# Operand tiles of a two-layer decoder kernel moved to per-stage byte offsets

## The chip, the cores and the metric

The kernel runs on one core of a Trainium2 chip. The metric is the device time of one execution in microseconds. A core has five engines that run side by side: TensorE (matmuls), VectorE, ScalarE, GpSimd and SyncE (which here only issues transfers). The profile calls them PE (PEld for its weight loads), DVE, ACT, POOL and SP. Operands lie in SBUF, a memory of 128 partitions; TensorE writes its sums to PSUM.

## What is computed

Two layers of a decoder over 256 tokens of width 1024, in float32: a mixer block with four branches and gates, a cross attention over 256 memory tokens, and an MLP. Each is added to the residual x.

```python
def reference(x, mem, positions, norm_mix, w_in, ...):
    for l in range(DEPTH):
        h = rmsnorm(x, norm_mix[l])
        x = x + mixer_block(h, positions, w_in[l], ...)
        x = x + cross_attention(rmsnorm(x, norm_xattn[l]), rmsnorm(mem, norm_mem[l]),
                                xattn_wq[l], xattn_wk[l], xattn_wv[l], xattn_wo[l])
        x = x + squared_relu_mlp(rmsnorm(x, norm_mlp[l]), w_up[l], w_down[l])
    return rmsnorm(x, norm_final)

def mixer_block(h, ...):
    zin = h @ w_in
    ...
    proj = jnp.einsum('bsnw,nwd->bsnd', branches, w_branch)
    gate = jax.nn.sigmoid(gates).reshape(b, s, N_BRANCH, D_MODEL)
    merged = jnp.sum(gate * proj, axis=2)
    return merged @ w_out

def squared_relu_mlp(h, w_up, w_down):
    a = jax.nn.relu(h @ w_up)
    return (a * a) @ w_down
```

w_in has 6840 columns (2744 for the four branches and 4096 for the gates), w_up and w_down have 1024 x 4096 weights. Nearly all the work is products of the 256 tokens with these weights.

## The kernel before

**Activations and products.** Activations lie transposed: the channel on the partition, 256 tokens along it, two blocks of 128 channels in one tile of 128 x 2 x 256 floats (2048 bytes in a partition). Products are made to nearly float32 accuracy from three matmuls in a narrower format, float32r: each operand is split into a high part and the rest, and `mm3` (line 188) adds high x high, high x low and low x high into one PSUM bank. So for each block of 128 x 128 weights there are three matmuls with 256 columns, and each of them has its own weight load (LDWEIGHTS) ahead of it:

```python
def mm3(out, ah, al, bh, bl, start, stop):
    PE.matmul(out, ah, bh, start=start, stop=False)
    PE.matmul(out, ah, bl, start=False, stop=False)
    PE.matmul(out, al, bh, start=False, stop=stop)
```

In `gemm` (line 207) the weights are the stationary side and the activations move: one half of a weight transfer (128 x 1024) holds eight blocks, and is followed by 24 matmuls. In `gemm_tok` (line 237) the activations are stationary and the weights move, with 512 columns in a matmul; it is used for a part of w_in, for the cross attention's values and for the last product of the second layer.

**Weights.** `half` (line 166) takes half of a transfer of 1 MB from the buffers `wr` (three of them, issued by SyncE in order), lets ScalarE write the high part `wh` and VectorE the rest `wl`. There are four buffers of each, 4096 bytes in a partition.

**Operands.** The other side of each product is split in the same way and lies in tiles named by the stage: `xh`, `xl` (normed x for w_in), `hh`, `hl` (for the gates, for the queries and for the MLP's w_up), `mh`, `ml` (memory for keys and values), `brh`, `brl` (branches), `mgh`, `mgl` (merged, for w_out), `oh`, `ol` (attention, for the output weights), `ah`, `al` (the MLP's hidden layer, for w_down). Other products among tiles, `kx` with `qx` and `ph` with `vx` in the cross attention, and small products in full float32 (`cst` with `sq` in `stat`, line 340, among others) stand between the large ones.

**Where tiles lie.** Each pool is a stretch of SBUF, and the tiles of a pool follow each other. Pool `cp` has constants and x. Pool `wp` has three `wr` of 8192 bytes, then four `wh` and four `wl` of 4096. Pool `ap` begins with a pad of `PAD` = 48 floats (line 123), and then has only tiles of 2048 bytes: 44 pieces that `new` (line 88) hands out and `rel` takes back, eight tiles for gates (`gate_tile`, line 350, which also hold `xh` and `xl` of a layer's first product), and eight for `hh` and `hl`, made once in layer 0 (lines 1051 to 1054) and written anew for each of their three stages. At the bottom of SBUF, ahead of all pools, 16,384 bytes of each partition are kept by default for descriptors of transfers that GpSimd issues.

**Order.** In a layer the stages are: w_in (`ev_dn`, `zin_rest`), then the mixers, written as generators whose pieces alternate, while the gates' products follow (`gates`, line 1075); then the keys of the cross attention (`mh`), `merge` (`brh`), w_out (`mgh`), the queries (`hh`), the attention, its output product (`oh`), w_up (`hh`) and w_down (`ah`). A scheduler orders the instructions by the program's order and by raised priorities (`urgent`, `high_priority`); each engine then runs its own list and waits at semaphores. `operands` (line 353), called where a residual is added, writes the split operands of the stage that follows.

## Time and profile before

| | |
|---|---|
| runs | 1099.88 and 1101.76 us, median 1100.82 us |
| profiled execution | 1099.05 us |
| its span, first to last instruction | 1097.3 us |
| mean granted TensorE clock | 0.997 |
| busy: PE, PEld | 1072.7 us (98%), 1028.3 us (94%) |
| busy: DVE, ACT, POOL | 812.4 us (74%), 583.7 us (53%), 196.2 us (18%) |
| matmuls recorded | 8494 |
| transferred | 185.13 MB, mean 169 GB/s |

The page of a profile gives one execution: the busy time of each engine, the chain of work that ended last with its share by engine and line, the costliest groups of instructions (line, engine, operation, output and inputs by name, shape, count, busy time, mean duration, and the idle time ahead of them), and the transfers. Other views cut out windows of time, list instructions in order of time, or list who waited for whom. A name such as `g<-hh,wl` says that a PSUM tile `g` is written from the moving operand `hh` and the stationary operand `wl`. Matmuls overlap: the next one starts before the last one has ended, so a matmul's duration is longer than its share of the time.

### The profile page before, as it was taken

Reading aid. Unit: us, or ns where it says so; the run is one execution under the profiler, and the core shown is the slowest. Engines: PE = TensorE matmul, PEld = TensorE weight load, DVE = VectorE, ACT = ScalarE, POOL = GpSimd, SP = SyncE. Lnnn points to the kernel's source line nnn. Section 1 sums busy time; section 2 is a strip of 40 time slices with the busy share of each in tenths; the row PEclk is TensorE's granted clock in tenths of the full one; section 3 lists DMA queues with packets and bytes.
Section 4 is the critical chain, followed back from the end, with each engine's and each line's share of the span. In section 5 each row is a group of like instructions: output and inputs, shape, how many; then the busy total and the mean of one; then the engine's idle time right before and its main releaser. Section 6 shows DMA issues by size and latency. Waiting matters only on the chain.

```text
span 1097.3 us, 20696 instructions
## 1 busy us (share of the span) xinstructions
PE 1072.7 (98%) x8494; PEld 1028.3 (94%) x8494; DVE 812.4 (74%) x1419; ACT 583.7 (53%) x875; POOL 196.2 (18%) x170
## 2 busy tenths in 40 slices
PE   8989999999999999999999999999999999999996
PEld 8979998899998999999999899999999899999885
DVE  7999858789865966655679997586797778665454
ACT  6565554554654655544454746554455555555342
POOL 6334005108200200000101420320361001010000
PEclk9999999999999999999999999999999999999998
DMA  9442623354543555555555444244555345554551
GB/s 368 169 173 98 224 86 123 106 193 174 182 151 148 182 185 179 188 190 192 192 183 192 155 151 156 85 166 136 191 188 197 119 151 193 192 205 161 194 189 39
DMA packets 28319, 185.13 MB, mean 169 GB/s; under 512 B 3392, under 2 KB 3648, under 8 KB 6976
## 3 DMA queue, kind: packets, MB, share of 16 engines
q1 hardware_dynamic: 26208, 179.09, 45.0%
q10 hardware_dynamic: 2016, 4.72, 1.3%
q8 instruction: 66, 1.08, 0.4%
q14 instruction: 29, 0.24, 0.1%
HBM read 182.75 MB, written 1.05 MB: 168 GB/s over the span
## 4 chain that ended last, share of the span: by engine, by line
PE 80%; DVE 11%; ACT 3%; DMA 3%; issue 1%; POOL 1%; ACTq 0%; DVEq 0%; POOLq 0%
PE g L189 24%; PE g L191 24%; PE g L190 24%; DVE wl L185 3%; DMA mr<-memt 2%; DVE qt L846 1%; PE ps L189 1%; ACT wh L182 1%; PE ps L191 1%; PE ps L190 1%; DVE gt L1097 1%; PE ps L652 1%; PE ps L648 1%; DMA wr<-ws 1%; DVE mgl L1105 1%
## 5 line engine op out<-in xcount | busy, mean ns | idle before, releaser
L185 DVE TENSOR_TENSOR wl<-wr,wh 128x1024 fp32r<-128x1024 f32 (+1 forms) x337 | 416.0, 1237 | 188.3 <-ACT wh L182 186.7
L182 ACT ACTIVATE wh<-wr 128x1024 fp32r<-128x1024 f32 (+1 forms) x337 | 354.9, 1056 | 343.0 <-PE g L190 241.7
L191 PE MATMUL g<-hh,wl 128*128 128x256 f32 x1152 | 325.4, 283 | 3.5 <-DVE wl L185 3.5
L189 PE MATMUL g<-hh,wh 128*128 128x256 f32 x1152 | 324.1, 282 | 2.1 <-ACT gt L1082 1.5
L190 PE MATMUL g<-hl,wh 128*128 128x256 f32 x1152 | 323.2, 281 | 0.0
L191 PEld LDWEIGHTS g<-hh,wl 128*128 128x128 f32 x1152 | 217.0, 188 | 5.4 <-DVE wl L185 4.3
L189 PEld LDWEIGHTS g<-hh,wh 128*128 128x128 f32 x1152 | 217.2, 189 | 3.3 <-ACT gt L1082 2.0
L190 PEld LDWEIGHTS g<-hl,wh 128*128 128x128 f32 x1152 | 218.4, 190 | 0.4 <-issue 0.2
L329 POOL TENSOR_TENSOR sq<-sq,sq 128x512 f32<-128x512 f32 x14 | 22.1, 1580 | 350.0 <-ACT sq L321 349.8
L189 PE MATMUL g<-xh,wh 128*128 128x256 f32 x272 | 75.2, 281 | 1.2 <-ACT xh L302 1.2
L190 PE MATMUL g<-xl,wh 128*128 128x256 f32 x272 | 75.8, 281 | 0.3 <-DVE xl L311 0.3
L191 PE MATMUL g<-xh,wl 128*128 128x256 f32 x272 | 74.9, 280 | 0.0
L189 PE MATMUL g<-ah,wh 128*128 128x256 f32 x256 | 72.0, 281 | 0.0
L190 PE MATMUL g<-al,wh 128*128 128x256 f32 x256 | 72.0, 281 | 0.0
L191 PE MATMUL g<-ah,wl 128*128 128x256 f32 x256 | 72.0, 281 | 0.0
L189 PEld LDWEIGHTS g<-xh,wh 128*128 128x128 f32 x272 | 51.0, 189 | 1.6 <-ACT xh L302 1.6
L190 PEld LDWEIGHTS g<-xl,wh 128*128 128x128 f32 x272 | 51.2, 189 | 0.5 <-DVE xl L311 0.5
L1098 POOL TENSOR_TENSOR gt<-gt,gt 128x512 f32<-128x512 f32 x16 | 35.5, 2217 | 89.9 <-DVE gt L1097 89.0
L191 PEld LDWEIGHTS g<-xh,wl 128*128 128x128 f32 x272 | 50.8, 189 | 0.0
L191 PE MATMUL g<-wh,al 128*128 128x512 f32 x128 | 50.1, 394 | 0.0
L190 PE MATMUL g<-wl,ah 128*128 128x512 f32 x128 | 49.9, 392 | 0.0
L189 PE MATMUL g<-wh,ah 128*128 128x512 f32 x128 | 49.4, 389 | 0.0
(500 smaller groups left out, 2333.7 us busy)
## 6 DMA issues: line engine op xcount, KB each, us to landing
wr<-ws SPq DMA_DIRECT2D x166, 1024.0 KB, 4.8
wr<-ws ACTq DMA_DIRECT2D x4, 512.0 KB, 7.5
mr<-memt ACTq DMA_DIRECT2D x8, 256.0 KB, 4.7
par<-par SPq DMA_DIRECT2D x2, 778.0 KB, 7.0
x<-xt SPq DMA_DIRECT2D x3, 256.0 KB, 7.6
cst<-cst SPq DMA_DIRECT2D x1, 588.0 KB, 8.7
gf<-fin SPq DMA_DIRECT2D x2, 256.0 KB, 5.3
yt<-yg ACTq DMA_DIRECT2D x2, 256.0 KB, 2.5
```

The costliest lines, as they stand in the source:

```text
L182: i = S.activation(wh[:, p], r[:, p], AF.Copy)
L185: V.tensor_tensor(wl[:, p], r[:, p], wh[:, p].bitcast(F32), op=ALU.subtract)
L189: PE.matmul(out, ah, bh, start=start, stop=False)
L190: PE.matmul(out, ah, bl, start=False, stop=False)
L191: PE.matmul(out, al, bh, start=False, stop=stop)
L329: G.tensor_tensor(acc, acc, sq, op=ALU.add)
L648: PE.matmul(xp[:, h], M[:, h], Tm[:, h], start=True, stop=True)
L652: PE.matmul(up[:, h], X[t][:, h], U[:, h], start=True, stop=True)
L846: V.tensor_tensor(qt[:, a].rearrange("p (b h) -> p b h", h=h), e3, halves(qbd[a // 2][:, a % 2], i)[:, :, 1], op=ALU.mult)
L1097: V.scalar_tensor_tensor(gt[m][a], gt[m][a], 1.0, ps, op0=ALU.add, op1=ALU.mult)
L1098: G.tensor_tensor(gt[m][0], gt[m][0], gt[m][1], op=ALU.add)
L1105: V.scalar_tensor_tensor(dl, t, 0.5, dh.bitcast(F32), op0=ALU.mult, op1=ALU.subtract)
```

## The change

The change gives the operands of each stage a byte offset within their tile, from a table with one row per layer. To make room for it, each of the 60 tiles of pool `ap` (pieces, gate tiles and tiles of h) becomes 128 bytes longer, 2176 instead of 2048. The 7,680 bytes that this takes come from the reserve at the bottom of SBUF, which goes from 16,384 to 1,024 bytes.

- `place` makes a tile of 512 + 32 floats and returns a view of it that begins at the given byte.
- `new` and `gate_tile` look the name up in the row of the layer that `lay` holds; names that are not in the table begin at 0. Where before `xl` was a name of its own, both parts of x are now looked up as `xh`.
- `hplace` makes the eight tiles of h once and returns views at the offset of the stage: `gate` before the gates, `q` before the product whose residual writes the queries' operands, `up` before the one that writes those of w_up.
- `lay` is set at the start of a layer, and to the next layer just before w_down of layer 0, as its residual writes the next layer's `xh`.

No instruction is added to the program or taken from it.

```diff
+SLACK = 128
+PLACE = [
+    dict(xh=16, gate=112, mh=8, ml=8, brh=120, brl=120, mgh=32, mgl=32, q=96, oh=48, ol=48, up=16, ah=112, al=112),
+    dict(xh=112, gate=8, mh=16, ml=16, brh=112, brl=112, mgh=4, mgl=4, q=124, oh=64, ol=64, up=120, ah=16, al=16),
+]
...
+    lay = [0]
+
+    def place(dt, shape, tag, name, byte):
+        t = ap.tile([P, 512 + SLACK // 4], dt, tag=tag, name=name)
+        n = int(np.prod(shape[1:]))
+        v = t[:, byte // 4 : byte // 4 + n]
...
+        return v
+
     def new(dt=F32, shape=(P, 2, T), name="a"):
...
-        t = ap.tile(list(shape), dt, tag=f"pc{i}", name=nm(name))
+        t = place(dt, shape, f"pc{i}", nm(name), PLACE[lay[0]].get(name, 0))
...
+    hf, hv = [], {}
+
+    def hplace(stage):
+
+        if not hf:
+            for j in range(4):
+                hf.append([ap.tile([P, 512 + SLACK // 4], F32R, tag=f"h{n}{j}", name=nm("h" + n)) for n in "hl"])
+        o = PLACE[lay[0]][stage] // 4
+        for n in range(2):
+            hv[n] = [t[n][:, o : o + 512].rearrange("p (a b) -> p a b", a=2) for t in hf]
+        return hv[0], hv[1]
...
     def gate_tile(i, dt=F32, name="gt"):
-        return ap.tile([P, 2, T], dt, tag=f"gt{i}", name=nm(name))
+        return place(dt, (P, 2, T), f"gt{i}", nm(name), PLACE[lay[0]].get(name, 0))
...
-            dh, dl = (Norm.h[j], Norm.l[j]) if mix else (hh[j], hl[j])
+            dh, dl = (Norm.h[j], Norm.l[j]) if mix else (hv[0][j], hv[1][j])
...
-        if l == 0:
-            for j in range(4):
-                for d, n in ((hh, "hh"), (hl, "hl")):
-                    d.append(ap.tile([P, 2, T], F32R, tag=f"{n}{j}", name=nm(n)))
+        hh, hl = hplace("gate")
+        H, L = ch(hh), ch(hl)
...
+        hh, hl = hplace("q")
+        H, L = ch(hh), ch(hl)
         gemm(ch(mgh), ch(mgl), 8, 4, residual(gain(4 * l + 1)), lead=True, tail=True)
...
+        hh, hl = hplace("up")
+        H2, L2 = ch(hh), ch(hl)
         gemm(ch(oh), ch(ol), 8, 4, residual(gain(4 * l + 3)), lead=True, tail=True)
...
-        gemm(H, L, 8, 16, ev_up, lead=True)
+        gemm(H2, L2, 8, 16, ev_up, lead=True)
         if l + 1 < NL:
+            lay[0] = l + 1
             gemm(ch(ah), ch(al), 32, 4, residual(gain(4 * l + 4), True, rrow), tail=True)
...
-    nc = _bacc.Bacc("TRN2", target_bir_lowering=False, num_devices=1)
+    nc = _bacc.Bacc("TRN2", target_bir_lowering=False, num_devices=1, dynamic_dma_scratch_size=1024)
```

## The prediction

> **What bounds the kernel now.** I read the page first: engine totals, chain that ended last, costliest groups.

> ```profile
> span 1097.3 us, 20696 instructions
> ...
> PEclk9999999999999999999999999999999999999998
> ...
> PE 80%; DVE 11%; ACT 3%; DMA 3%; issue 1%; POOL 1%; ACTq 0%; DVEq 0%; POOLq 0%
> ...
> L191 PE MATMUL g<-hh,wl 128*128 128x256 f32 x1152 | 325.4, 283 | 3.5 <-DVE wl L185 3.5
> ```

> The reader is to see that TensorE carries the chain, at the full granted clock, and that its work is one kind of matmul: three per 128x128 block of weights (lines 189 to 191), 256 columns each. They number 3 x 1152 with h, by the loops 3 x 272 with xh, 3 x 256 with ah, and 384 each with mh, br, mg and oh: 6576. The wait view says how little else there is. Its largest rows are these, and all its rows make some 15 us.

> ```profile
> PE g L191 <- DVE wl L185: 3.5, 4, 1.0
> PE ps L693 <- DVE s L690: 1.6, 1, 1.6
> ```

> So the time is the number of matmuls times the step from one to the next. A duration of 283 ns is no step, since two or three matmuls are in flight. The step comes from the windows view (window, its length, TensorE's busy time and count): the length over the count less 2.4, for the matmuls that began before the window (283 over 118).

> ```profile
> 39.00:59.00 20.00, 20.00 (x172) 1.00 0.49 170
> 267.50:290.00 22.50, 22.50 (x192) 1.00 0.53 198
> 290.50:313.00 22.50, 22.50 (x194) 1.00 0.51 184
> 377.60:462.40 84.80, 84.80 (x723) 1.00 0.53 188
> 462.60:553.00 90.40, 90.40 (x770) 1.00 0.52 186
> 553.40:576.00 22.60, 22.60 (x194) 1.00 0.49 184
> 831.60:849.00 17.40, 17.40 (x150) 1.00 0.59 207
> 913.80:998.50 84.70, 84.70 (x722) 1.00 0.54 196
> 811.00:829.00 18.00, 18.00 (x161) 1.00 0.55 212
> 769.00:783.00 14.00, 14.00 (x126) 1.00 0.52 200
> 648.00:657.00 9.00, 9.00 (x82) 1.00 0.33 115
> 889.00:907.00 18.00, 18.00 (x161) 1.00 0.40 131
> 103.00:112.00 9.00, 9.00 (x79) 1.00 0.13 43
> 632.00:644.00 12.00, 12.00 (x104) 1.00 0.47 175
> 759.00:767.00 8.00, 8.00 (x70) 1.00 0.36 133
> 313.20:317.70 4.50, 4.50 (x40) 1.00 0.46 131
> 849.30:853.90 4.60, 4.60 (x41) 1.00 0.39 137
> 607.00:617.00 10.00, 10.00 (x45) 1.00 0.52 179
> 1001.00:1087.00 86.00, 86.00 (x377) 1.00 0.40 147
> ```

> The first eight rows (w_in of layer 0 late, w_out and q of layer 0, up, down, w_in of layer 1, q and up of layer 1) are one speed: 90.40 / (770 - 2.4) = 117.8 ns, 84.70 / (722 - 2.4) = 117.7; where the quotient is above that, a short wait is in it. The next four are another: 18.00 / (161 - 2.4) = 113.5, then 113.3, 113.1, 113.5; I call it 113.4. The three after them, in the mixer stages, are at the first speed again (117.5, 118.1, 118.3). The two rows of kx with qx are a third: 119.7 and 119.2. The last two, with 512 columns, come back in part (3). Clock and instruction are the same in all; only operands and history differ. The timeline shows where the speed changes:

> ```profile
> 375.87 0.28 PE L190 MATMUL g<-hl,wh 128*128 128x256 f32 x1
> 375.98 0.28 PE L191 MATMUL g<-hh,wl 128*128 128x256 f32 x1
> 376.10 0.50 PE L343 MATMUL ps<-cst,sq 128*128 128x1 f32 x4
> ...
> 376.89 0.28 PE L191 MATMUL g<-hh,wl 128*128 128x256 f32 x1
> 377.01 0.28 PE L190 MATMUL g<-hl,wh 128*128 128x256 f32 x1
> 377.13 0.28 PE L191 MATMUL g<-hh,wl 128*128 128x256 f32 x1
> ```

> Steps of 0.11 before four small products of the norm, of 0.12 after them, and then 117.8 through all of up and down. The speed is a pace (113.4 the quick one, 117.8 the long one) that lasts until something else runs on TensorE. The products come in threes, and three steps take 340, 353 and 359 ns: the quick pace plus none, two and three hitches of some 6.5 ns. [...]

> **The change, part by part.** In the kernel before, the sizes of the weight buffers and of the pieces are multiples of 128 bytes and the pad between them is 192, so every operand lies 64 bytes past such a multiple, counted from the weights. With the table the distance modulo 128 is 64 plus the entry. Layer 0: xh 80, gate 48, mh 72, br 56, mg 96, q 32, oh 112, up 80, ah 48. Layer 1: xh 48, gate 72, mh 80, br 48, mg 68, q 60, oh 0, up 56, ah 80. A piece of 2176 bytes is 17 x 128, and the smaller reserve at the bottom moves everything by 15,360 = 120 x 128 bytes; so tiles without an entry keep their distance, and kx with qx (both pieces, distance 0) stay at 119.7.

> What a new distance does to the step, no row shows. The bounds from rows are 113.4, the quick pace, and 119.7, distance 0. I take 113.4: distance 64 reaches it for whole stages, and is thrown out of it only by what comes between, so a distance that suits a stage needs only to keep it there.

> (1) The first eight rows hold 3117 matmuls, 3100 without those that began before. 3100 x (117.8 - 113.4) = 13.6 us, all on the path, as TensorE waits for nothing there. Bounds: that, or 3100 x (119.7 - 117.8) = 5.9 us lost.

> (2) The other 3476 alternate. Of the seven windows quoted of them (811 to 767 in the list, 88 us) three are at the long pace, 29 us: a third, so 1150 x 4.4 = 5.1 us. Some of it meets a wait; I take 4. Bounds: 5.1 won, or, from a mean of 114.9, 3476 x (119.7 - 114.9) = 17 us lost.

> (3) The matmuls in which the weights are the moving side have 512 columns: 86.00 / (377 - 1.7) = 229.1 ns in the last gemm (384 by its loop), 231 in the window of w_in of layer 1, which I take for all other 288. Twice the quick step is 226.8, so 0.9 + 1.2 = 2.1 us at best; nothing at worst, or the same lost again. I take 1.0.

> (4) oh of layer 1 goes to distance 0, that of kx with qx, and runs at the quick pace now (889 to 907). 192 x (119.7 - 113.5) = 1.2 us lost; 0 if the place keeps the quick pace.

> (5) No instruction is added: the place calls only make views, and the three places of h lie in the tiles that h had before, so the same waits order them. ScalarE and VectorE write the same elements from another start, under this cover (PE, PEld, DVE, ACT, POOL):

> ```profile
> 388.00:557.00 169.00, 169.00 (x1437) 169.00 (x1437) 103.73 (x106) 84.19 (x100) 6.44 (x5) 1.00 0.52 186
> ```

> VectorE is busy 61% of the densest stretch, ScalarE 50%, the DMA engines 52%. At 113.4 these become 64, 52 and 54%, no bound yet, and writes slower by a tenth would still leave TensorE the last. Large transfers all go through queues that SP and ACT issue, none by POOL, so I cost the smaller reserve at nothing:

> ```profile
> q1 hardware_dynamic: 26208, 179.09, 45.0%
> ...
> wr<-ws SPq DMA_DIRECT2D x166, 1024.0 KB, 4.8
> ```

> Were transfers slower for it, three buffers of two halves each stand against a landing of 4.8 us; one buffer lasts 48 x 113.4 ns = 5.4 us.

> Sum: -13.6 - 4 - 1.0 + 1.2 = -17.4 us. The profiled execution took 1099.05 us (span 1097.3 and 1.75 around it), 1.8 below the median of the runs shown. So 1081.7 on its scale, 1083 on that of the runs, which I take.

> **The rivals.**

> B, half of it. What comes between still throws stages into the long pace, though others than now. For it: w_out has the long pace in layer 0 (267 to 290) and the quick one in layer 1 (811 to 829), from the same code at the same distance. Half of 17.4 us: 1091.

> C, no effect. History alone decides, distance nothing; some stages swap paces, and the time stays within 4 us of 1100. For it: the same two rows. Against it: kx with qx, which lie at another distance, have another speed, the same in both layers. [...]

> D, slower. A start that is no multiple of 64 bytes costs each matmul one more hitch, the 119.7 step, whatever the pace. The mean step is now (3100 x 117.8 + 3476 x 114.9) / 6576 = 116.3, so with a share s at 119.7 and the rest at 113.4 the gain is gone at s = 2.9 / 6.3 = 0.46. With all there, 6576 x 3.4 = 22 us are lost, and 2 more in the 512-column stages: 1125. For it: every entry but that of oh in layer 1, 64, leaves the grid of 64 bytes, and no row shows such a start; against it: nothing. [...]

> E, below the quick step. 113.4 may hold a hitch itself, as the rungs 113.4, 117.8 and 119.7 need not begin with the lowest. One matmul in three without a hitch of 6.5 ns is 2.2 ns a step, 6576 x 2.2 = 14 us more: 1069; all of them without it, 1040. For it: only the spacing of the rungs. Against it: no quoted window of 256 columns is under 113.

> **How the numbers follow.** The forecast has 0.44, with a range of its own from 1077 (parts 1 to 3 at their best, no loss at oh) to 1088 (part 1 two thirds done); B 0.19, C 0.14, D 0.10, E 0.13. The range 1070 to 1101 leaves out D, most of E and the upper end of C. A measurement of this kernel tells about 2%, 22 us, from no change: below 1078.8 lie E and a quarter of the forecast, 0.24; above 1122.8 half of D, 0.05; the rest is 0.71.

> **What would show it.** The forecast: the windows of up, down and w_in of layer 1, now at 117.8, come out at 113.4, and the step is the same before and after the norm's four products. Part (4): oh of layer 1 at 119.7. Part (5): the DVE, ACT and DMA rows unchanged. B shows as stages at two speeds, others than now; C as a mean step of 116.3; D as 119 or more in most stages; E as any long window under 113. The ground of it is wrong if a stage's speed differs from piece to piece of one operand: neighbouring pieces, now 2176 bytes apart, alternate modulo 256, so that the pattern would repeat at 256 bytes and not at 128.

## The result and the profile after

The changed kernel takes 1113.04 us (1112.35 and 1113.73), against 1100.82: a ratio of 1.0111, 95% interval 1.0065 to 1.0157. It is a loss of about 12 us where the forecast had a gain of 17, and it lies above the range of the forecast, which ended at 1101. The number of instructions is the same, 20696. These are the lines of the page after; the line numbers have moved, and `mm3` is now at 218 to 220:

```profile
span 1110.4 us, 20696 instructions
...
PE 1088.0 (98%) x8494; PEld 1043.6 (94%) x8494; DVE 812.7 (73%) x1419; ACT 584.3 (53%) x875; POOL 195.9 (18%) x170
...
PE 88%; DVE 6%; ACT 2%; DMA 2%; issue 1%; POOL 0%; DVEq 0%; ACTq 0%
...
L220 PE MATMUL g<-hh,wl 128*128 128x256 f32 x1152 | 326.0, 283 | 3.2 <-DVE wl L214 3.2
...
wr<-ws SPq DMA_DIRECT2D x166, 1024.0 KB, 4.8
```

TensorE's busy time rose by 15.3 us for the same 8494 matmuls, and every other engine's total stayed within 0.7 us. The mean of one matmul, 283 ns, says nothing of it, as before. Nor did a large new wait appear; these are the two largest of TensorE's waits, and the same two cost 3.5 and 1.2 us before:

```profile
PE g L220 <- DVE wl L214: 3.2, 4, 0.8
PE g L218 <- ACT xh L331: 2.0, 1, 2.0
```

The whole time without a matmul, span less busy time, fell from 24.6 to 22.4 us. So the loss is in the step. The windows view of TensorE in the changed kernel shows it, read as in the prediction: the length over the count less 2.4 (1.7 in the last row, with 512 columns).

```profile
382.00:466.00 84.00, 84.00 (x715) 1.00 0.52 185
470.00:557.00 87.00, 87.00 (x738) 1.00 0.51 184
925.00:1009.00 84.00, 84.00 (x703) 1.00 0.51 184
815.00:834.00 19.00, 19.00 (x159) 1.00 0.50 174
225.00:245.00 20.00, 20.00 (x170) 1.00 0.57 203
892.00:916.00 24.00, 24.00 (x206) 1.00 0.35 121
838.00:857.00 19.00, 19.00 (x164) 1.00 0.46 168
653.50:662.50 9.00, 9.00 (x78) 1.00 0.26 97
318.00:322.00 4.00, 4.00 (x36) 1.00 0.32 100
1020.00:1100.00 80.00, 80.00 (x347) 1.00 0.40 145
```

The steps, in the order of the rows, with the step of the same stage in the kernel before in brackets: up of layer 0 117.9 ns (117.7), down 118.3 (117.8), up of layer 1 119.9 (117.7), w_out of layer 1 121.3 (113.5), keys of layer 0 119.3, oh of layer 1 117.9 (113.5), q of layer 1 117.6 (118), mixers 119.0 (113.1), kx with qx 119.0 (119.7), last product 231.7 (229.1). The granted clock is 1.00 in all of them, before and after. No stage has the quick pace any more.

The mean by stage can be had from the start times of all matmuls in the trace, from one start to the next (steps of 135 ns and more, in which something else stands between, are left out, and so are ten of under 30 ns). Over the 256-column matmuls it goes from 116.35 to 118.57 ns. Times the number of matmuls, the stages of the prediction's part (1) lose 4.6 us, the rest of the 256-column stages 11.0, of which oh of layer 1 has 0.9, and the 512-column ones 1.2. That makes 16.8; with 2.2 us less without a matmul 14.6 remain, against 13.1 in the span. The other 1.5 us I can't place.

### The profile page after: what moved, and what is told of

Read it like the earlier page. It is cut to its first block, busy times and chain, and to the rows that moved or that the text cites. A ratio compares the mean times of both kernels' runs of the same rounds, so it can differ in the third digit from the quotient of the medians.

```text
span 1110.4 us, 20696 instructions
## 1 busy us (share of the span) xinstructions
PE 1088.0 (98%) x8494; PEld 1043.6 (94%) x8494; DVE 812.7 (73%) x1419; ACT 584.3 (53%) x875; POOL 195.9 (18%) x170
## 3 DMA queue, kind: packets, MB, share of 16 engines
q1 hardware_dynamic: 26208, 179.09, 44.7%
## 4 chain that ended last, share of the span: by engine, by line
PE 88%; DVE 6%; ACT 2%; DMA 2%; issue 1%; POOL 0%; DVEq 0%; ACTq 0%
PE g L218 26%; PE g L219 26%; PE g L220 26%; DVE wl L214 2%; DMA mr<-memt 1%; PE ps L218 1%; PE ps L219 1%; PE ps L220 1%; DVE qt L875 1%; ACT wh L211 1%; PE ps L677 1%; PE ps L681 1%; DMA wr<-ws 0%; PE ps L986 0%; DVE sp L530 0%
## 5 line engine op out<-in xcount | busy, mean ns | idle before, releaser
L218 PE MATMUL g<-xh,wh 128*128 128x256 f32 x272 | 76.2, 284 | 2.0 <-ACT xh L331 2.0
L219 PE MATMUL g<-xh,wh 128*128 128x256 f32 x272 | 76.5, 283 | 0.0
L218 PEld LDWEIGHTS g<-xh,wh 128*128 128x128 f32 x272 | 51.4, 190 | 2.4 <-ACT xh L331 2.4
L219 PEld LDWEIGHTS g<-xh,wh 128*128 128x128 f32 x272 | 51.4, 189 | 0.1
## 6 DMA issues: line engine op xcount, KB each, us to landing
wr<-ws SPq DMA_DIRECT2D x166, 1024.0 KB, 4.8
```

## Experiments

The operands' distance from the weights' buffers is given below modulo 256 bytes where the tiles of pool `ap` lie a multiple of 256 apart. There the base (table entry 0) is 192, the same as in the kernel before, whose tiles are 2048 = 8 x 256 apart. Diffs are against the changed kernel. Each time is a median; each ratio is to the kernel before, run on the same chip.

### Spacing and offsets apart

The change does two things: tiles 2176 bytes apart instead of 2048, and offsets from a table. Three kernels take them apart. `spacing_2176` keeps the spacing, with all offsets 0:

```diff
-PLACE = [
-    dict(xh=16, gate=112, mh=8, ...
+ZERO = dict(gate=0, q=0, up=0)
+PLACE = [ZERO, ZERO]
```

> Tiles 2176 bytes apart as in the change, every offset of the table 0, so all operands stay 64 past a multiple of 128 from the weights. Theory S (the spacing does it: the pattern that decides the step repeats at 256 bytes or more, and neighbouring tiles that alternate break the quick pace): 1109 to 1114 us, no stage below 117 ns a step. Theory O (the offsets do it: a distance other than 64 modulo 128 takes the quick pace away): 1101 us within 4, w_out of layer 1 and oh at 113.4 as before, and kx with qx at 119.8.

`spacing_2304` makes the room 256 bytes as well, so that tiles are 2304 = 9 x 256 apart:

```diff
-SLACK = 128
+SLACK = 256
+ZERO = dict(gate=0, q=0, up=0)
+PLACE = [ZERO, ZERO]
```

> Tiles 2304 = 9 x 256 bytes apart, every offset 0. Theory S with a period of 256: as before the change, 1101 us within 4, with stages at 113.4 and 117.8. Theory S with a longer period (512 or more): 1107 to 1114, no stage at 113.4. Theory O: 1101 within 4.

`table_2304` keeps the offsets of the change, with tiles 2304 apart:

```diff
-SLACK = 128
+SLACK = 256
```

> The change with 256 instead of 128 bytes of room: its offsets, but tiles 9 x 256 bytes apart. Theory S with a period of 256: the gain that the offsets may bring is seen alone, under 1105 us, with stages at 113.4. Theory O: as the change, 1109 to 1116 us, steps of 117.8 to 121.5 by stage (121 for w_out of layer 1 at distance 68).

| kernel | tiles apart | offsets | us | ratio, 95% |
|---|---|---|---|---|
| spacing_2304 | 2304 | none | 1099.31 | 0.9999 (0.9990 to 1.0008) |
| spacing_2176 | 2176 | none | 1103.57 | 1.0046 (1.0029 to 1.0063) |
| table_2304 | 2304 | the table | 1113.79 | 1.0136 (1.0120 to 1.0151) |
| the change | 2176 | the table | 1113.04 | 1.0111 (1.0065 to 1.0157) |

The windows of up and down of layer 0 and up of layer 1, first in `spacing_2304`:

```profile
377.00:461.00 84.00, 84.00 (x716) 1.00 0.52 188
465.00:552.00 87.00, 87.00 (x741) 1.00 0.53 185
913.00:997.00 84.00, 84.00 (x716) 1.00 0.53 192
```

then in `table_2304`:

```profile
381.00:466.00 85.00, 85.00 (x716) 1.00 0.50 183
470.00:557.00 87.00, 87.00 (x738) 1.00 0.52 184
925.00:1010.00 85.00, 85.00 (x710) 1.00 0.52 185
```

In the first they are the steps of the kernel before (117.7, 117.8, 117.7), and the ratio is 0.9999. So the room and the smaller reserve cost nothing here. In the second they are 119.1, 118.3 and 120.1: most of the loss comes with the offsets. But 128 bytes of spacing alone, with no offset, cost 0.46%. The time of `spacing_2176` is that of theory O, its steps are mostly those of theory S: w_out of layer 1 has 117.6 ns from start to start, where theory O kept the quick pace. Oh of layer 1 has the quick pace with tiles 2304 apart (24.00 us for 212 matmuls, 114.5 ns) and not with 2176 (206 in 24.00 us, 117.9). The two losses don't add up. One reading, which no run here tests, is that where nothing has the quick pace any more, the spacing has little left to take.

### Is it the period?

2176 bytes make neighbouring pieces alternate between two distances modulo 256, the case that the prediction named as its ground failing. `low_128` makes the distance alternate in another way. Tiles are 2304 apart, the high parts stay at 192, and the low parts go 128 bytes further, to 64:

```diff
-SLACK = 128
+SLACK = 256
+ZERO = dict(gate=0, q=0, up=0, xl=128, ml=128, brl=128, mgl=128, ol=128, al=128)
+PLACE = [ZERO, ZERO]
...
-            hv[n] = [t[n][:, o : o + 512].rearrange(...
+            hv[n] = [t[n][:, o + 32 * n : o + 32 * n + 512].rearrange(...
...
-            ... Norm.l.append(gate_tile(2 * j + 1, F32R, "xh"))
+            ... Norm.l.append(gate_tile(2 * j + 1, F32R, "xl"))
```

> Tiles 9 x 256 bytes apart, the high parts at offset 0, the low parts 128 bytes further in their tiles. Theory A (neighbours 2176 bytes apart alternate modulo 256, and high and low parts then meet the weights at different places): the quick pace is gone and the time is near that of spacing_2176, 1103 to 1108 us, steps of 117 to 118. If 128 is the period and alternation means nothing: as spacing_2304, 1098 to 1102 us, with stages at 113.4.

1107.05 us, ratio 1.0067 (1.0050 to 1.0084). Both 192 and 64 are distances at which stages ran at the quick pace when all operands of the stage shared one of them (113.5 ns in w_out of layer 1 before, 114.0 in up of layer 0 in `scan_a` below). With one for the high part and one for the low part none did: the mean step is 117.8 ns, without a quick stage. 192 and 64 are the same modulo 128, so in this run the step did not go by the distance modulo 128.

### Other distances

`pad_208` is the kernel before with another pad ahead of pool `ap`, so that every operand moves alike (this diff is against the kernel before):

```diff
-PAD = 48
+PAD = 52
```

> The kernel before with a pad of 208 instead of 192 bytes: tiles 2048 apart, all operands at distance 80 modulo 128, one of the distances of the table. Theory S: the spacing is untouched, so two paces remain, 1097 to 1105 us. Theory O: no quick pace, every large stage at 117 to 118.5 ns, 1107 to 1114 us.

1111.30 us, ratio 1.0114 (1.0099 to 1.0129). The pad didn't become 208 bytes: the addresses in the built program show 224. The distance was therefore 224 modulo 256 (96 modulo 128) and not the 80 of the expectation. At it both paces are gone: up and down of layer 0 run at 118.2 and 118.4 ns. One move of all operands alike, with no spacing and no table, costs as much as the change.

`scan_a` and `scan_b` put the stages at many distances, all of them multiples of 16:

```diff
-SLACK = 128
+SLACK = 256
 PLACE = [
# scan_a
+    dict(xh=128, gate=192, mh=80, brh=144, mgh=176, q=208, oh=240, up=128, ah=160, ...
+    dict(xh=192, gate=128, mh=48, brh=224, mgh=96, q=80, oh=96, up=96, ah=128, ...
# scan_b
+    dict(xh=96, gate=96, mh=128, brh=128, mgh=128, q=128, oh=128, up=224, ah=96, ...
+    dict(xh=224, gate=240, mh=192, brh=192, mgh=208, q=240, oh=208, up=176, ah=96, ...
```

> Tiles 9 x 256 bytes apart, every stage at a distance of its own modulo 256 (192 is the distance before the change). Layer 0: xh 64, gates 128, mh 16, br 80, mg 112, q 144, oh 176, up 64, ah 96; layer 1: xh 128, gates 64, mh 240, br 160, mg 32, q 16, oh 32, up 32, ah 64. Theory P (128 bytes are the period, and 64 in it is the one place with a quick pace): the stages at 64 step at 113.4 or 117.8 ns as before, all others between 116.5 and 121.5, 1102 to 1112 us. Theory Q (the period is 256 and 192 alone has the quick pace): the stages at 64 have no 113.4 either, and those at 128 are not like those at 0, 1106 to 1114 us.

> The same with other distances. Layer 0: xh 32, gates 32, mh, br, mg, q and oh 64, up 160, ah 32; layer 1: xh 160, gates 176, mh and br 128, mg 144, q 176, oh 144, up 112, ah 32. Theory P: mh, br, mg, q and oh of layer 0 step as in the kernel before (113.4 or 117.8), mh and br of layer 1 at 120 like distance 0, 32 at 116.7 as in the queries of table_2304, and 160 like 32; 1100 to 1110 us. Theory Q: none at 113.4, 160 unlike 32, 1104 to 1114 us.

1105.54 us (1.0051, 1.0031 to 1.0072) and 1104.30 us (1.0039, 1.0023 to 1.0055). Up of layer 0 (distance 64) and down (96) in `scan_a`:

```profile
380.00:460.00 80.00, 80.00 (x704) 1.00 0.54 196
...
466.00:550.00 84.00, 84.00 (x702) 1.00 0.52 185
```

and up of layer 1 (112) in `scan_b`:

```profile
920.00:1000.00 80.00, 80.00 (x708) 1.00 0.55 199
```

They are 114.0, 120.1 and 113.4 ns: distance 112 gave the quick pace to a stage that ran at the long one in the kernel before, but for its first 38 matmuls. Neither theory had expected a quick stage at 112. Two kernels then put whole layers at the four distances that lie 16 bytes from a multiple of 128; 112, 16 and 144 had each shown a quick stage in the scans. A third and a fourth test the table's entries as distances. The first, `all_112_16`, has layer 0 at 112 and layer 1 at 16; `all_144_240` has 144 and 240:

```diff
-SLACK = 128
+SLACK = 256
 PLACE = [
# all_112_16: every entry of layer 0, of layer 1
+    dict(xh=176, gate=176, ...
+    dict(xh=80, gate=80, ...
# all_144_240
+    dict(xh=208, gate=208, ...
+    dict(xh=48, gate=48, ...
```

> Tiles 9 x 256 bytes apart, all operands of layer 0 at distance 112 modulo 256 from the weights, all of layer 1 at 16. Theory R (16 bytes on either side of a multiple of 128 are places where the quick pace holds, as up of layer 1 did at 112 and mh of layer 0 at 16): up and down of layer 0 and up of layer 1 at 113.4, 1080 to 1092 us. Theory H (the scans met the quick pace by what ran before those stages): stages at both paces as before, 1096 to 1108 us.

> The same with 144 for layer 0 and 240 for layer 1, the other two places 16 bytes from a multiple of 128. Theory R: as all_112_16, 1080 to 1092 us. Theory H: 1100 to 1112 us, since q and mg at 144 and mh at 240 stepped at 117 to 119 in the scans.

1093.08 us (0.9942, 0.9924 to 0.9960) and 1103.13 us (1.0037, 1.0024 to 1.0051). Layer 0 at 112 is quick throughout. Layer 1 at 16 is not; here are its up and its w_out in `all_112_16`:

```profile
905.00:985.00 80.00, 80.00 (x707) 1.00 0.55 193
804.00:822.00 18.00, 18.00 (x153) 1.00 0.60 221
```

113.5 and 119.5 ns, and the time lies between the two ranges expected. Distances 16 and 144 turn out to have two paces, as 64 and 192 have, and they change within a stage. Up of layer 1 at 16 begins with 38 matmuls at a mean of 118.7 ns from start to start and goes on at 113.3 after the norm's four products; up of layer 0 at 144 begins at 113.3 and goes on at 118.7. Distance 240 has no quick stage (117.2).

`table_base0` and `table_base0_2304` have the table's entries themselves as distances, the pad being a multiple of 256:

```diff
-PAD = 48
+PAD = 64
# table_base0_2304 also
-SLACK = 128
+SLACK = 256
```

> The change with a pad of 256 bytes instead of 192, so that an entry of the table is itself the distance modulo 128 (xh 16, gates 112, up 16, ah 112 in layer 0, and so on), tiles 2176 apart. Theory R and a table meant as distances: most stages near 113.4 in spite of the spacing, 1080 to 1095 us. If the offsets do no good at any base: 1103 to 1114 us.

> The same with tiles 9 x 256 bytes apart. Theory R: as table_base0 or better by the 4 us that the spacing of 2176 cost alone, 1078 to 1092 us. If the offsets do no good at any base: 1100 to 1112 us.

1114.28 us (1.0138, 1.0122 to 1.0154) with tiles 2176 apart, 1103.55 us (1.0042, 1.0028 to 1.0056) with 2304. The 1080 to 1095 us of theory R did not come. With this base the spacing alone is worth 11 us. In the second kernel up (16) and down (112) of layer 0, up (120) and w_out (4) of layer 1 are:

```profile
381.00:461.00 80.00, 80.00 (x705) 1.00 0.53 186
466.00:548.00 82.00, 82.00 (x726) 1.00 0.54 194
915.00:1000.00 85.00, 85.00 (x704) 1.00 0.52 182
808.00:826.00 18.00, 18.00 (x149) 1.00 0.60 219
```

113.9, 113.3, 121.2 and 122.8 ns: the quick pace at two distances on the grid of 16 bytes, and the slowest steps yet at two off it.

### One distance for all, and its two controls

`all_112` has every stage at 112 with tiles 2304 apart. Only `ah` of layer 1 has 240: in the last product weights and activations change sides, so that the weights, which move there, lie 16 bytes past the activations.

```diff
-SLACK = 128
+SLACK = 256
 PLACE = [
+    dict(xh=176, gate=176, mh=176, ... ah=176, al=176),
+    dict(xh=176, gate=176, mh=176, ... ah=48, al=48),
```

> Tiles 9 x 256 bytes apart, all operands of both layers at distance 112 modulo 256, and those of the last product, where the weights move, at 240, so that the weights lie 16 past them. If 112 holds the quick pace for every stage, as layer 0 of all_112_16 did: large stages at 113.4 to 115 ns in both layers, the last product at 226.7, 1080 to 1085 us. If that was a matter of layer 0's order of work: layer 1 at both paces, 1086 to 1094 us.

`all_112_2176` has the same distance modulo 128, with the change's spacing (`SLACK` stays at 128):

```diff
 PLACE = [
# both layers
+    dict(xh=48, gate=48, mh=48, ... ah=48, al=48),
```

> All operands at distance 112 modulo 128, the last product's too, but tiles 2176 bytes apart as in the change. If alternation modulo 256 breaks any good place: no stage at 113.4, 1098 to 1110 us. If a good place survives it: 1082 to 1090 us, as all_112.

`off_16_bytes` has the spacing of `all_112`, with layer 0 moved by 8 bytes to 120 and layer 1 by 4 to 116:

```diff
-SLACK = 128
+SLACK = 256
 PLACE = [
+    dict(xh=184, gate=184, ...
+    dict(xh=180, gate=180, ...
```

> Tiles 9 x 256 bytes apart, all operands of layer 0 at distance 120, all of layer 1 at 116: 8 and 4 bytes past the 112 of all_112, and off a grid of 16 bytes. If such starts cost a hitch of their own: no stage under 118, those of layer 1 at 120 to 123, 1115 to 1135 us. If 8 bytes matter little: 1082 to 1095 us.

| kernel | us | ratio, 95% |
|---|---|---|
| all_112 | 1085.52 | 0.9857 (0.9840 to 0.9873) |
| all_112_2176 | 1107.76 | 1.0060 (1.0045 to 1.0075) |
| off_16_bytes | 1127.65 | 1.0241 (1.0225 to 1.0256) |

`all_112` is faster than both kernels of the study. The page of its profile:

```profile
span 1084.7 us, 20696 instructions
...
PE 1061.2 (98%) x8494; PEld 1015.9 (94%) x8494; DVE 811.8 (75%) x1419; ACT 584.3 (54%) x875; POOL 196.5 (18%) x170
```

TensorE's busy time is down by 11.5 us against before and 26.8 against the change, with the same instructions. The windows of up and down of layer 0, up and oh of layer 1, and the last product in `all_112`:

```profile
377.00:457.00 80.00, 80.00 (x708) 1.00 0.53 192
462.00:544.00 82.00, 82.00 (x726) 1.00 0.54 194
905.00:985.00 80.00, 80.00 (x708) 1.00 0.56 199
874.00:897.00 23.00, 23.00 (x203) 1.00 0.31 116
995.00:1075.00 80.00, 80.00 (x352) 1.00 0.40 145
```

113.4, 113.3, 113.4, 114.7 (a short wait among them; 113.8 from start to start) and 228.4 ns. And the timeline of `all_112` at the place where the kernel before fell into the long pace, the four products of the norm:

```profile
375.12 0.28 PE L219 MATMUL g<-hl,wh 128*128 128x256 f32 x1
375.23 0.28 PE L220 MATMUL g<-hh,wl 128*128 128x256 f32 x1
375.35 0.50 PE L372 MATMUL ps<-cst,sq 128*128 128x1 f32 x4
...
376.15 0.28 PE L220 MATMUL g<-hh,wl 128*128 128x256 f32 x1
376.27 0.28 PE L219 MATMUL g<-hl,wh 128*128 128x256 f32 x1
376.39 0.28 PE L220 MATMUL g<-hh,wl 128*128 128x256 f32 x1
376.51 0.28 PE L218 MATMUL g<-hh,wh 128*128 128x256 f32 x1
376.62 0.28 PE L219 MATMUL g<-hl,wh 128*128 128x256 f32 x1
376.74 0.28 PE L220 MATMUL g<-hh,wl 128*128 128x256 f32 x1
376.85 0.28 PE L218 MATMUL g<-hh,wh 128*128 128x256 f32 x1
376.96 0.28 PE L219 MATMUL g<-hl,wh 128*128 128x256 f32 x1
377.08 0.28 PE L220 MATMUL g<-hh,wl 128*128 128x256 f32 x1
```

Steps of 0.12 follow the four products here too, but from 376.74 on three steps take 0.34, the quick pace again. So what comes between disturbs the pace at 112 as well; the difference is that the pace comes back. After such a break the steps in `all_112` are 114 to 121 ns for up to 14 matmuls. Of the 49 stretches of 25 steps or more without a break, none ends at the long pace (its last ten steps at a mean over 115.5 ns); in the kernel before 24 of 50 do, and down is at the long pace throughout. The same three stages of up and down in `all_112_2176`:

```profile
380.00:464.00 84.00, 84.00 (x716) 1.00 0.50 184
470.00:554.00 84.00, 84.00 (x717) 1.00 0.51 187
920.00:1005.00 85.00, 85.00 (x724) 1.00 0.54 195
```

and in `off_16_bytes`:

```profile
385.00:471.00 86.00, 86.00 (x713) 1.00 0.50 178
476.00:564.00 88.00, 88.00 (x729) 1.00 0.51 181
938.00:1025.00 87.00, 87.00 (x708) 1.00 0.51 179
```

117.7, 117.5 and 117.8 ns in the one. Half of its tiles now lie at 240, where a whole layer of `all_144_240` had 117.2; mixed with 112, the step is longer than at either alone, and the time 22 us longer than that of `all_112`. 121.0, 121.1 and 123.3 in the other: 8 bytes cost 6.7% of the step, 4 bytes 8.7%.

## Why the prediction was wrong

**What bounds the kernel: right.** The time is the number of matmuls times the step. Every kernel here has the same matmuls at the same clock (means of 0.995 to 0.998 over the runs), and the medians, from 1085.5 to 1127.7 us, follow the mean step, from 114.1 ns in `all_112` to 121.5 in `off_16_bytes`.

**The step that failed is the value for the new distances.** "I take 113.4: distance 64 reaches it for whole stages, and is thrown out of it only by what comes between, so a distance that suits a stage needs only to keep it there." In the change the stages came to 117.7 to 121.5 ns instead, from start to start, and none to 113.4. The same instruction had the quick pace at a few distances and not at the others. From start to start, these are the mean steps of stages at one distance throughout (modulo 256; tiles a multiple of 256 apart):

| distance | mean step, ns |
|---|---|
| 112 | 113.3 to 115.1, all stages |
| 64, 192 | 113.5 to 117.8, two paces |
| 16, 144 | 113.6 to 118.7, two paces |
| 32, 240 | 116.7 to 117.3 |
| 160, 208 | 117.3 to 118.5, 117.8 to 119.2 |
| 48, 80, 128, 224 | 118.3 to 119.1 |
| 176 | 119.2 |
| 0, 96 | 120.0 |
| off the grid of 16: 60; 8, 124 | 116.7; 118.2 to 118.9 |
| 56, 196, 200 | 119.8 to 120.4 |
| 4, 116, 120 | 120.9 to 123.2 |

The prediction had rows of only two distances, 64 and 0 modulo 128, and a quick pace in one of them; its bounds, 113.4 and 119.7, held within 0.3 ns for every multiple of 16, but it took the end that suited the forecast. Nothing in the trace of before told where between them a new distance would lie, and the value in the middle of the two, 116.6, would have forecast no change.

**The ground that the pattern repeats at 128 failed too**, as the prediction said it might: "neighbouring pieces, now 2176 bytes apart, alternate modulo 256". `spacing_2176` against `spacing_2304`, and `all_112_2176` against `all_112`, show its price, 4 and 22 us. With it falls "tiles without an entry keep their distance": kx with qx left 119.7 for 118 to 119, as one of its tiles now lay 128 bytes elsewhere.

**The sum.** Part (1), −13.6, came out at +4.6 in the change; in `all_112`, where its assumption holds, the same stages win 13.9. So its working was sound and its premise was not. Part (2), −4, came out at +11.0, the oh of part (4) among it. The matmuls that had the quick pace lost it, and w_out of layer 1 (entry 4), the keys (8) and the merge of layer 0 (120) went to 119.4 to 121.5. Even in `all_112` part (2) is worth only 1.1: the mean of its stages, 114.9 before as the prediction had it, becomes 114.5 and not 113.4, because other matmuls break into these stages often, and the steps after a break are long at 112 too (114 to 121 ns in `all_112`). Part (3), −1.0, came out at +1.2, and `all_112` has +0.2. Two numbers of the prediction's working are off without changing the outcome: the matmuls with xh are 864, not 816, which changes part (2) by about 0.1 us, and parts (1) to (3) at their best, 20.8 us, lead to 1080 and not to 1077.

**Part (4)**, oh of layer 1 at distance 0, was right where the distance is one distance: 119.9 ns from start to start in `table_2304`, a loss of 1.2 us as worked out. In the change, with alternating pieces, it is 118.2, or 0.9 us.

**Part (5) was right.** The window over up and down of layer 0 in the changed kernel, and the row of one of VectorE's largest writes of an operand with an offset, which had a mean of 692 ns before as well:

```profile
397.00:566.00 169.00, 169.00 (x1435) 169.00 (x1434) 102.68 (x111) 84.04 (x100) 6.46 (x5) 1.00 0.53 190
```

```profile
L1242 DVE TENSOR_TENSOR al<-up,ah 128x512 fp32r<-128x512 f32 x32 | 22.1, 692 | 1.8 <-ACT ah L1241 1.8
```

The writers, the transfers and the smaller reserve cost nothing here: the write takes its 692 ns, the transfers of `wr` land in 4.8 us as before, and `spacing_2304`, with the smaller reserve, has the ratio 0.9999. The starts of `al` are multiples of 16 here; in `off_16_bytes`, where they are not, the same write has a median of 693 ns.

**The rivals.** D had the sign, and its form was close: steps at 119 and above, and 1125 us if all stages had them, where `off_16_bytes` takes 1127.65. But its grid of 64 bytes is wrong: 112 lies off it and is quick in every stage, 0 and 128 lie on it and are not. The change lay between D and "no change", as stages with two thirds of its matmuls came to 117.7 to 118.4 and the others to 119.4 to 121.5. B is out, as no stage has the quick pace. C is wrong as to distance and right in one thing: at 192 the distance alone does not decide. The prediction's timeline shows it within one stage, with steps of 0.11 us before the norm's four products and 0.12 after them; and from the kernel before to `spacing_2304`, with the same distances, w_out of layer 0 went from 117.8 to 114.5 ns and the merge from 114.0 to 117.0, while the time stayed. E did not show: no stage with 256 columns has a mean under 113.3.

Addresses alone moved the time by 42 us, from 1085.52 in `all_112` to 1127.65 in `off_16_bytes`. No run here shows whether the weight loads, which run beside the matmuls (94% busy in both kernels of the study), have a part in the longer steps. The slowest steps, 120.9 to 123.2 ns at 4, 116 and 120, are off the grid of 16 bytes, but so is 60, where q of layer 1 in `table_2304` had 116.7 ns.

**What stays open.** Why 112 suits every stage (113.3 to 115.1 ns) and 144, its mirror, does not (113.6 to 118.7, together with 16); and why tiles 2304 bytes apart cost nothing (0.9999) where 2176 cost 4 and 22 us. Whether the distance counts or the moving operand's own start is settled for distance 0 alone. There kx and qx, both among the pieces, stepped at 119.6 to 120.0 ns with both starts at 192, at 224 (`pad_208`) and at 0 (`table_base0_2304`) modulo 256, while starts at 192 beside weights at 0 had 113.5 to 117.8. For every other distance the weights lie at multiples of 256 in all kernels here, so start and distance can't be told apart, off the grid of 16 above all. That was not tried. The hitches of 6.5 ns by which the prediction counted, two of them in three steps at the long pace, are not shown, and the single steps speak against them: in down of the kernel before each takes 116 to 120 ns, in `all_112` 113 or 114.

## What to carry to other kernels

Where one engine has no waits and all its instructions are alike, measure the step from start to start, by stage, and look for different steps at one clock before looking for anything else. If there are some, try one distance between moving and stationary operands for the whole kernel, with all tiles of both sides a multiple of 256 bytes apart (112 bytes past the weights was worth 1.4% here, and with tiles 2176 apart lost 0.6%); change spacing and offset one at a time. The price at one address said nothing of another here (113.4 ns at 112, 121.0 at 120): with rows of two distances only, the forecast belongs in the middle of its bounds.
